# A SwiGLU down projection as seven block products, with the weights' sums made during the up projections

## The chip, the cores and the metric

One core of a Trainium2 chip runs one launch of the kernel. The metric is the device time of one execution in microseconds; lower is better. The time before is the median of three runs.

## The reference

Two layers of a decoder trunk with 512 tokens and a width of 1024, all in f32. In each layer one projection feeds four branches (a gated convolution, sparse attention with an indexer and a choice of the 128 best keys, a gated linear recurrence, and attention to 256 memory tokens). Each branch is lifted to the full width, gated and summed; an output projection and a residual follow, then a SwiGLU feed-forward network with a residual:

```python
x = x + merged @ w_out
hf = rmsnorm(x, norm_ffn)
gate, up = jnp.split(hf @ ffn_w_up, 2, axis=-1)        # 1024 -> 2 x 2816
return x + (jax.nn.silu(gate) * up) @ ffn_w_down        # 2816 -> 1024
```

The change is in the last line of the second layer: a product of (512 x 2816) with (2816 x 1024).

## The kernel before

**Precision.** TensorE multiplies in a rounded form of f32 (f32r). So each operand is split into a high part, a copy rounded by ScalarE (ACT, L97), and a low part, the difference that VectorE (DVE) takes. `mm3` (L271 to L276) makes of each block product three matmuls into one PSUM bank: high by high (L274), high by low (L275), low by high (L276).

**Weights.** `wchunk` (class `Chunk`, L212) loads up to 2048 columns per partition (1 MB) from DRAM by SP's queue into one of two `w_raw` buffers; ACT makes `w_hi` and DVE makes `w_lo` (L229) in parts of 1024 columns, three buffers of each. The profile calls both by these names.

**PSUM.** Eight banks of 128x512 f32: three for `mm` (projections), three for `tr` (transposes and norms) and two for `at` (attention). In the mixer `values` (L681) accumulates four token tiles at once and uses the three `mm` banks and one of `at`; meanwhile the attention's dots (L702, L703, exponentials on L715) use the `at` banks too.

**Order.** The program is written in Tile, and a planner with its own timeline of the engines sets the order of the instructions on each engine ahead of time. Each engine works off its list in order. `tc.high_priority` draws an instruction forward in the plan. Buffers and their semaphores order what the engines do with one another.

**The feed-forward network**, `ffn` (L1058). The hidden width of 2816 is 11 chunks of 256, in two parts of six and five chunks (each followed by its share of the down projection, so that the activations of one part fit in SBUF). For each chunk two 1 MB weight blocks make gate and up in feature-major form (96 matmuls of 128x512), DVE scales them by the norm as it evicts them (`fg`, `fu`, L1081), ACT applies Silu, DVE multiplies (L1086), and the product is split into `a_hi` (ACT) and `a_lo` (DVE, L1088).

The down projection of a part that isn't the last of layer 2 is `residual` (L1021): pairs of 128 output features, weights stationary, all chunks of the part accumulated in one bank for each, and added to `xT` (L1035), the residual stream that stays in SBUF, feature-major. In part 0 of layer 2 every finished feature block is also transposed (`transposed`, L1067) into `x_tok`, token-major. Part 1 of layer 2 is `final` (L1045): four token tiles by 512 columns accumulate in the three `mm` banks and one of `at`, activations stationary, are added to `x_tok` (L1051) and go out: the left 512 columns in one DMA (1 MB), the right ones in pieces of 128x256 by the queues of SP and ACT. In layer 1 the last part also spills x to DRAM (`x_spill`), from where the next mixer's end loads it again.

Of the kernel before, what the change touches and what calls it, by code (L numbers as in the profile page):

```python
# [12 lines left out]
F32 = mybir.dt.float32  # L13
F32R = mybir.dt.float32r
# [7 lines left out]
P = 128  # L22
# [47 lines left out]
def hybrid_trunk(ctx: ExitStack, tc: tile.TileContext, x, mem, positions, norm_mix, w_in, conv_w,  # L70
# [41 lines left out]
    def f(ap):  # L112
        return ap.bitcast(F32)

    ident = consts.tile([P, P], F32, name="ident")
    make_identity(nc, ident)
# [9 lines left out]
    dve.memset(one, 1.0)  # L126
    neg = consts.tile([P, P], F32, name="neg")
    dve.memset(neg, NONC)
# [141 lines left out]

    def mm3(ps, a, b, first, last):  # L271
        ah, al = a
        bh, bl = b
        pe.matmul(ps, ah, bh, start=first, stop=False)  # L274
        pe.matmul(ps, ah, bl, start=False, stop=False)  # L275
        pe.matmul(ps, al, bh, start=False, stop=last)  # L276

    x_dram = nc.dram_tensor("x_spill", [P, KD, S], F32, kind="Internal").ap()
    kv_dram = [nc.dram_tensor(f"kv{l}", [P, 4, 2, 2, MEM], F32, kind="Internal").ap() for l in range(DEPTH)]

# [21 lines left out]

    def column_means(ps, ones, sq, hi, lo):
        A(hi, sq, AF.Copy)
        dve.tensor_sub(lo, sq, f(hi))
        pe.matmul(ps, ones, hi, start=True, stop=False)
        pe.matmul(ps, ones, lo, start=False, stop=True)

    def norm_feature(ssq):
        ps = tr_ps()  # L310
        column_means(ps, ones_dr, ssq, *(scratch512(S).bitcast(F32R) for _ in range(2)))
# [172 lines left out]

    ones_dr = consts.tile([P, P], F32R, name="ones_dr")
    dve.tensor_copy(ones_dr, ones_d)
    ones_hr = consts.tile([P, P], F32R, name="ones_hr")
# [6 lines left out]
    a0, a1 = prm[:, 64:68], prm[:, 68:72]  # L494
    mx, e0, e1, sm, z0 = (small(H4, name=f"lb{i}", bufs=1) for i in range(5))
    dve.tensor_max(mx, a0, a1)
# [18 lines left out]

    def mixer(l, h, norms, cm, cf):
        mix = cm.enter_context(tc.tile_pool(name="mix", bufs=1, side="right"))
# [164 lines left out]
        def values(hv):  # L682
            ws = [wchunk(w_in[l][k0 * P:(k0 + 4) * P, C_GI:C_GI + 512], 4, 512) for k0 in (0, 4)]
            pss = [mm_ps() for _ in range(MM_BUFS)] + [at_ps()]
            tokens_wide(ws, h, KD, pss)
            for t, ps in enumerate(pss):
                with tc.high_priority(offset=AHEAD):
                    i = A(hv[:, t, :], ps, AF.Copy, scale=r_t[:, t:t + 1])
                if t < MM_BUFS:
                    behind.append(i)  # L690
            yield

        with pool_("dsa") as dp:
# [46 lines left out]
            with pool_("idx") as ip:  # L740
# [83 lines left out]
                def select(t):  # L824
                    n = (t + 1) * P
                    score = ip.tile([P, S], F32, name="score", bufs=1)[:, :n]
                    for hh in range(8):
# [9 lines left out]
                    dve.copy_predicated(score[:, t * P:], future, neg)  # L837
                    yield
# [22 lines left out]
                mgp = cf.enter_context(pool_("mgp", "left"))  # L861
                merged = mgp.tile([P, KD, S], F32, name="merged")
# [140 lines left out]

        res = cf.enter_context(tc.tile_pool(name="res", bufs=1))
        xT = res.tile([P, KD, S], F32, name="xT")
        for c in range(KD):
            nc.sync.dma_start(xT[:, c, :], x_dram[:, c, :])
        with pool_("outp") as op:
# [8 lines left out]
            residual(xT, w_out[l], mg, KD, 256, h2, ssq2, lambda c: g_ffn(l, c))  # L1017
        return h2, ssq2, xT

    def residual(xT, w2d, a, kt, cols, h2, ssq2, gain, spill=False, done=None):  # L1020
        for m0 in range(0, KD, cols // P):  # L1021
            ws = []
            k0 = 0
            per = 2048 // cols
            while k0 < kt:
                n = min(per, kt - k0)
                ws.append((k0, n, wchunk(w2d[k0 * P:(k0 + n) * P, m0 * P:m0 * P + cols], n, cols)))
                k0 += n
            pss = [mm_ps() for _ in range(cols // P)]
            for js in ([range(cols // P)] if m0 + cols // P < KD else [[j] for j in range(cols // P)]):  # L1030
                for k0, n, w in ws:
                    features(w, a, js, k0, kt, [pss[j] for j in js])
            for j in range(cols // P):
                m = m0 + j
                dve.tensor_add(xT[:, m, :], xT[:, m, :], pss[j])  # L1035
                if h2 is not None:
                    h_chunk(h2, ssq2, m, gain(m), xT[:, m, :])
                if spill:
                    nc.scalar.dma_start(x_dram[:, m, :], xT[:, m, :])
                if done is not None:  # L1040
                    done(m)

    def final(x_tok, w2d, a, kt):
        for m0 in range(0, D, 512):
            cols = slice(m0, m0 + 512)  # L1045
            ws = [wchunk(w2d[k0 * P:min(k0 + 4, kt) * P, cols], min(4, kt - k0), 512) for k0 in range(0, kt, 4)]
            pss = [mm_ps() for _ in range(MM_BUFS)] + [at_ps()]
            tokens_wide(ws, a, kt, pss)
            for t, ps in enumerate(pss):
                for c in ([cols] if m0 == 0 else [slice(m0 + e, m0 + e + 256) for e in (0, 256)]):  # L1050
                    dve.tensor_add(x_tok[:, t, c], x_tok[:, t, c], ps[:, c.start - m0:c.stop - m0])  # L1051
                    if m0:
                        q = nc.sync if c.start == m0 else nc.scalar
                        q.dma_start(out[0][t * P:(t + 1) * P, c], x_tok[:, t, c])
            if m0 == 0:
                nc.sync.dma_start(out[0][:, cols].rearrange("(t p) c -> p t c", p=P), x_tok[:, :, cols])

    def ffn(l, h, ssq, xT):  # L1058
        r_b = norm_feature(ssq)
# [3 lines left out]

        def transposed(m):
            ps = tr_ps()
            for t in range(NT):
                pe.transpose(ps[:, t * P:(t + 1) * P], xT[:, m, t * P:(t + 1) * P], ident)  # L1067
            A(x_tok[:, :, m * P:(m + 1) * P], ps.rearrange("p (a b) -> p a b", b=P), AF.Copy)

        with tc.tile_pool(name="ffn", bufs=1) as fp:  # L1070
            for f0, f1 in parts:
                kt = 2 * (f1 - f0)
                a = (fp.tile([P, 12, S], F32R, name="a_hi")[:, :kt], fp.tile([P, 12, S], F32R, name="a_lo")[:, :kt])
                for fc in range(f0, f1):
                    wg = wchunk(ffn_w_up[l][:, fc * 256:(fc + 1) * 256], KD, 256)
                    wu = wchunk(ffn_w_up[l][:, FF + fc * 256:FF + (fc + 1) * 256], KD, 256)
                    gs = [fp.tile([P, S], F32, name="fg", bufs=2) for _ in range(2)]
# [4 lines left out]
                    for j in range(2):  # L1082
                        i = 2 * (fc - f0) + j
                        g, u = gs[j], us[j]
                        A(g, g, AF.Silu)
                        dve.tensor_mul(g, g, u)  # L1086
                        A(a[0][:, i, :], g, AF.Copy)
                        dve.tensor_sub(a[1][:, i, :], g, f(a[0][:, i, :]))  # L1088
                wd = ffn_w_down[l][f0 * 256:f1 * 256, :]
                h2 = ssq2 = None  # L1090
                if last and f1 == n_f:
                    final(x_tok, wd, a, kt)
                    continue
                if f1 == n_f:
                    h2, ssq2 = new_h(), new_ssq()
                if last:
                    x_tok = fp.tile([P, NT, D], F32, name="x_tok")
                residual(xT, wd, a, kt, 256, h2, ssq2, lambda c: g_mix(l + 1, c), spill=h2 is not None,
                         done=transposed if last else None)
        return h2, ssq2  # L1100

    for l in range(DEPTH):
        with ExitStack() as ctx_ffn:
            with ExitStack() as ctx_mix:
                h, ssq, xT = mixer(l, h, (lambda: (norm_token(ssq), norm_feature(ssq))) if l else (lambda: norms),
                                   ctx_mix, ctx_ffn)
            h, ssq = ffn(l, h, ssq, xT)

# [28 lines left out]
```

## Time and profile before

| | us |
|---|---|
| median of 3 runs (lowest, highest) | 2047.54 (2046.99, 2047.55) |
| the profiled execution | 2047.71 |
| its span, first to last instruction | 2045.6 |
| layer 2, up projections of part 0 | from about 1687 to 1822 of the span |
| its down projection | to about 1887 |
| up projections of part 1 | to about 1987 |
| its down projection | to 2041.5 |
| last outputs | to 2045.6 |

A row of the profile has the start, the duration, the engine, the source line, the operation, what it writes and reads, and in brackets how long the engine had been idle and what released it. A group has count, total busy time, mean duration in ns, and the idle time before its instructions. A row of a DMA group has the queue, the count, the KB of each and the median microseconds from issue to landing. PE is TensorE, PEld its weight loads, POOL is GpSimd, SP is the engine whose queue loads the weights. The end of a matmul in the profile is modelled.

### The profile page before, as it was taken

Reading aid. Unit: us, or ns where it says so; the run is one execution under the profiler, and the core shown is the slowest. Engines: PE = TensorE matmul, PEld = TensorE weight load, DVE = VectorE, ACT = ScalarE, POOL = GpSimd, SP = SyncE. Lnnn points to the kernel's source line nnn. Section 1 sums busy time; section 2 is a strip of 40 time slices with the busy share of each in tenths; the row PEclk is TensorE's granted clock in tenths of the full one; section 3 lists DMA queues with packets and bytes.
Section 4 is the critical chain, followed back from the end, with each engine's and each line's share of the span. In section 5 each row is a group of like instructions: output and inputs, shape, how many; then the busy total and the mean of one; then the engine's idle time right before and its main releaser. Section 6 shows DMA issues by size and latency. Waiting matters only on the chain.

```text
span 2045.6 us, 26194 instructions
## 1 busy us (share of the span) xinstructions
PE 2031.7 (99%) x10156; PEld 1705.9 (83%) x10156; DVE 1277.0 (62%) x2519; ACT 1019.9 (50%) x1836; POOL 9.8 (0%) x33
## 2 busy tenths in 40 slices
PE   8999999999999999999999999999999999999999
PEld 8998987778888888888889898877888788888887
DVE  6779997657686544344457889864777654533442
ACT  7653655866665433223355456486766633322231
POOL 0000000000000000000000000000000000000000
PEclk9999999999999999999999999999999999999999
DMA  7623232212243232233243213222222422323222
GB/s 251 221 85 97 68 103 83 81 54 93 68 128 113 83 103 93 93 104 102 88 155 94 88 57 108 88 62 83 83 83 83 145 87 98 103 73 113 92 83 93
DMA packets 185660, 203.77 MB, mean 100 GB/s; under 512 B 4271, under 2 KB 172289, under 8 KB 185409
## 3 DMA queue, kind: packets, MB, share of 16 engines
q1 hardware_dynamic: 181248, 193.04, 29.7%
q10 hardware_dynamic: 4128, 8.93, 1.2%
q8 instruction: 80, 1.31, 0.3%
q14 instruction: 44, 0.35, 0.1%
q0 software_dynamic: 160, 0.13, 0.0%
HBM read 191.60 MB, written 10.49 MB: 99 GB/s over the span
## 4 chain that ended last, share of the span: by engine, by line
PE 97%; DMA 1%; DVE 1%; ACT 1%; issue 0%; SPq 0%; DVEq 0%
PE mm L274 29%; PE mm L275 29%; PE mm L276 29%; PE tr L732 1%; PE tr L726 1%; PE at L702 1%; PE at L703 1%; PE at L276 1%; PE at L274 1%; PE at L275 1%; DMA w_raw<-in_mem_w_kv_dram 1%; PE at L954 0%; PE at L980 0%; PE tr L668 0%; PE tr L771 0%
## 5 line engine op out<-in xcount | busy, mean ns | idle before, releaser
L229 DVE TENSOR_TENSOR w_lo<-w_raw,w_hi 128x1024 fp32r<-128x1024 f32 (+1 forms) x346 | 419.5, 1213 | 383.2 <-ACT w_hi L97 383.0
L274 PE MATMUL mm<-h_hi,w_hi 128*128 128x512 f32 x1664 | 651.9, 393 | 0.7 <-DVE fg L1081 0.4
L275 PE MATMUL mm<-h_lo,w_hi 128*128 128x512 f32 x1664 | 651.6, 392 | 0.0
L276 PE MATMUL mm<-h_hi,w_lo 128*128 128x512 f32 x1664 | 649.8, 392 | 0.0
L97 ACT ACTIVATE w_hi<-w_raw 128x1024 fp32r<-128x1024 f32 (+1 forms) x346 | 363.2, 1051 | 463.2 <-PE mm L275 397.5
L274 PEld LDWEIGHTS mm<-h_hi,w_hi 128*128 128x128 f32 x1664 | 313.2, 188 | 65.0 <-DVE fg L1081 1.2
L276 PEld LDWEIGHTS mm<-h_hi,w_lo 128*128 128x128 f32 x1664 | 312.9, 188 | 64.6 <-issue 0.6
L275 PEld LDWEIGHTS mm<-h_lo,w_hi 128*128 128x128 f32 x1664 | 313.1, 188 | 63.3 <-issue 1.0
L276 PE MATMUL mm<-w_hi,h_lo 128*128 128x256 f32 (+2 forms) x368 | 109.5, 298 | 0.0
L275 PE MATMUL mm<-w_lo,h_hi 128*128 128x256 f32 (+2 forms) x368 | 109.1, 297 | 0.0
L274 PE MATMUL mm<-w_hi,h_hi 128*128 128x256 f32 (+2 forms) x368 | 108.3, 298 | 0.0
L275 PE MATMUL mm<-a_lo,w_hi 128*128 128x512 f32 x272 | 106.1, 390 | 0.0
L274 PE MATMUL mm<-a_hi,w_hi 128*128 128x512 f32 x272 | 105.9, 389 | 0.0
L276 PE MATMUL mm<-a_hi,w_lo 128*128 128x512 f32 x272 | 105.6, 390 | 0.0
L274 PE MATMUL mm<-y_hi,w_hi 128*128 128x512 f32 x256 | 100.4, 393 | 1.2 <-ACT y_hi L97 1.2
L275 PE MATMUL mm<-y_lo,w_hi 128*128 128x512 f32 x256 | 100.7, 393 | 0.0
L276 PE MATMUL mm<-y_hi,w_lo 128*128 128x512 f32 x256 | 100.3, 392 | 0.0
L97 ACT ACTIVATE a_hi<-fg 128x512 fp32r<-128x512 f32 x44 | 27.8, 633 | 106.9 <-DVE fg L1086 106.9
L97 ACT ACTIVATE prob<-prob,small 128x256 f32<-128x256 f32 (+3 forms) x128 | 69.0, 554 | 14.7 <-DVE small L715 8.6
L275 PEld LDWEIGHTS mm<-w_lo,h_hi 128*128 128x128 f32 x368 | 70.2, 191 | 2.2
L276 PEld LDWEIGHTS mm<-w_hi,h_lo 128*128 128x128 f32 x368 | 70.2, 191 | 1.9
L274 PEld LDWEIGHTS mm<-w_hi,h_hi 128*128 128x128 f32 x368 | 69.9, 191 | 1.9
(377 smaller groups left out, 2982.9 us busy)
## 6 DMA issues: line engine op xcount, KB each, us to landing
w_raw<-in_w_in_dram SPq DMA_DIRECT2D x72, 1024.0 KB, 5.2
w_raw<-in_ffn_w_up_dram SPq DMA_DIRECT2D x44, 1024.0 KB, 5.1
w_raw<-in_w_lift_dram SPq DMA_DIRECT2D x32, 512.0 KB, 3.5
w_raw<-in_ffn_w_down_dram SPq DMA_DIRECT2D x16, 1024.0 KB, 5.3
w_raw<-in_mem_w_kv_dram SPq DMA_DIRECT2D x8, 1024.0 KB, 5.4
w_raw<-in_w_out_dram SPq DMA_DIRECT2D x8, 1024.0 KB, 5.4
w_raw<-in_ffn_w_down_dram SPq DMA_DIRECT2D x10, 512.0 KB, 3.4
kv<-kv ACTq DMA_DIRECT2D x8, 512.0 KB, 3.2
```

The lines of the kernel that those rows point to most:

```text
L97: i = act.activation(dst, src, func, **kw)
L229: dve.tensor_sub(lo, raw[:, k:e], f(hi))
L274: pe.matmul(ps, ah, bh, start=first, stop=False)
L275: pe.matmul(ps, ah, bl, start=False, stop=False)
L276: pe.matmul(ps, al, bh, start=False, stop=last)
L702: pe.matmul(ps, q[:, hh, s], k[0][:, :n], start=True, stop=False)
L703: pe.matmul(ps, q[:, hh, s], k[1][:, :n], start=False, stop=True)
L726: pe.transpose(pp[:, (2 * e + i) * P:(2 * e + i + 1) * P], probs[2 * i + e][:, b * P:(b + 1) * P], ident)
L732: pe.matmul(pv[e * HD:(e + 1) * HD, :], vt[:, b, :], pt[:, b, e * 2 * P:(e + 1) * 2 * P], start=b == 0, stop=b == t)
```

## The change

**Seven products.** Layer 2's down projection is computed for each chunk of 256 hidden features as a two-by-two block product: the activations as two halves of the tokens (256) by two halves of the chunk (128), the weights as two halves of the chunk by two halves of the columns (512). Eight block products become seven, on sums and differences of blocks: `A11`, `A12`, `A22`, `S1` to `S4` of the activations, and five of the weights' blocks and sums. Every block product is two token tiles of three matmuls of 128x512. The seven accumulate over all chunks of a part, in six banks (two `mm`, one `mm` with one `tr`, two `at`), in three phases; between the phases DVE adds banks into the output sum `acc`, and the accumulation goes on in the same bank where a later result contains an earlier one.

**Operands.** `operands` takes a chunk's two activation tiles and makes the seven blocks with their high and low parts. `weight_sums` loads the 256 rows of a chunk of `w_down` (1 MB) by POOL's queue into a third raw buffer, `w_raw7`, makes four sums in place on DVE and stores them in DRAM (`w_sums`), by POOL's queue again; one is made before each chunk's up projections. In the down projection SP's queue loads blocks of `w_down` and of `w_sums` into `w_raw` and `w_raw7` in turn.

**The residual stream.** x isn't held in SBUF through the network. The mixer's `residual` always spills it (ACT's queue); layer 1's down projection, `add_down`, loads each feature block by POOL's queue, adds and spills it again; layer 2 loads it in two 1 MB pieces into `w_raw7` by POOL's queue (`x_in`) and transposes it after chunks 1 and 3 of part 0.

**Banks.** `values` takes its fourth bank from `tr`.

Some constants are smaller, some pools lie elsewhere, and `fg` has three buffers. The core of the diff:

```diff
         def values(hv):
...
-            pss = [mm_ps() for _ in range(MM_BUFS)] + [at_ps()]
+            pss = [mm_ps() for _ in range(MM_BUFS)] + [tr_ps()]
...
+    def raw_tile(fp, turn=[0]):
+        turn[0] += 1
+        if turn[0] % 3 == 0:
+            return fp.tile([P, 2048], F32, name="w_raw7")
+        return wpool.tile([P, 2048], F32, name="w_raw", bufs=RAW_BUFS)
+
+    def split(srcs, earlier=()):
+        hi, lo = (wpool.tile([P, 2, 512], F32R, name=nm, bufs=W_BUFS) for nm in ("w_hi", "w_lo"))
+        with tc.high_priority(offset=AHEAD):
+            for k, n, src in srcs:
+                A(hi[:, k:k + n, :], src, AF.Copy)
+                follow(dve.tensor_sub(lo[:, k:k + n, :], src, f(hi[:, k:k + n, :])), earlier)
+        return [(hi[:, k, :], lo[:, k, :]) for k in range(2)]
+
+    def weight_sums(fp, w2d, i):
+        raw = fp.tile([P, 4, 512], F32, name="w_raw7")
+        nc.gpsimd.dma_start(raw.rearrange("p (e c) n -> p e (c n)", e=2),
+                            w2d[2 * i * P:2 * (i + 1) * P, :].rearrange("(e p) n -> p e n", p=P))
+        b12, b11, b22, b21 = (raw[:, j, :] for j in range(4))
+        dve.tensor_sub(b11, b12, b11)
+        dve.tensor_sub(b12, b22, b12)
+        dve.tensor_sub(b22, b22, b11)
+        dve.tensor_sub(b21, b21, b22)
+        nc.gpsimd.dma_start(wt_dram[:, i], raw)
+
+    def operands(fp, g0, g1):
+        hi, lo = (fp.tile([P, 7, HALF], F32R, name=nm, bufs=6) for nm in ("a_hi", "a_lo"))
+        def put(o, n, src):
+            h_, l_ = (x[:, o:o + n, :].rearrange("p a b -> p (a b)") for x in (hi, lo))
+            A(h_, src, AF.Copy)
+            dve.tensor_sub(l_, src, f(h_))
+        put(A11, 1, g0[:, :HALF])
+        put(A12, 2, g1)
+        dve.tensor_add(g0[:, HALF:], g0[:, HALF:], g1[:, HALF:])
+        dve.tensor_sub(g0[:, :HALF], g0[:, HALF:], g0[:, :HALF])
+        both = g1.rearrange("p (a b) -> p a b", b=HALF)
+        dve.tensor_sub(both, both, g0[:, None, :HALF].to_broadcast([P, 2, HALF]))
+        put(S2, 2, g0)
+        put(S4, 2, g1)
+        return hi, lo
+
+    def down(fp, w2d, sums, ops, evict):
+        n = len(ops)
+        b0 = mm_ps()
+        ba, bb, bc = [mm_ps(), mm_ps()], [b0, tr_ps()], [at_ps(), at_ps()]
...
+        for i0 in range(0, n, 2):
+            m = min(2, n - i0)
+            raw = raw_of(2 * m)
+            nc.sync.dma_start(raw, w2d[2 * i0 * P:2 * (i0 + m) * P, C1].rearrange("(k p) n -> p k n", p=P))
+            for i in range(m):
+                p1, p2 = split([(0, 2, raw[:, 2 * i:2 * i + 2, :])])
+                prod(ba, i0 + i, A11, p1, i0 + i == 0, i0 + i == n - 1)
+                prod(bb, i0 + i, A12, p2, i0 + i == 0, i0 + i == n - 1)
+        added = evict(ba, 0, C1) + evict(bb, 0, C1, True)
...
+        for i in range(n):
+            raw = raw_of(3)
+            nc.sync.dma_start(raw, sums[:, i, SUM1:])
...
+                todo = [(bc, S1, q5, j == 0, False), (ba, S2, q6, False, True), (bb, A22, q4, j == 0, False)]
...
+        added = evict(ba, 0, C2) + evict(bc, 2, C2)
+        later = added + evict(bb, 2, C1)
...
+            nc.sync.dma_start(raw[:, 0::2, :], sums[:, i0:i0 + m, SUM3])
+            nc.sync.dma_start(raw[:, 1::2, :], rows[:, i0:i0 + m, 1, C2])
...
+                p7, p3 = split([(0, 2, raw[:, 2 * i:2 * i + 2, :])], added if k == 1 else later if k else ())
+                prod(ba, k, S3, p7, False, k == n - 1, True)
+                late.append((bc, k, S4, p3, False, k == n - 1, True))
...
+        evict(ba, 2, C2, True)
+        evict(ba, 2, C1, True)
+        evict(bc, 0, C2, True, True)
...
+            def x_in(m0):
+                xs = fp.tile([P, 2048], F32, name="w_raw7")
+                nc.gpsimd.dma_start(xs.rearrange("p (m t) -> p m t", t=S), x_dram[:, m0:m0 + 4, :])
+                for m in range(4):
+                    ps = tr_ps()
+                    for t in range(NT):
+                        pe.transpose(ps[:, t * P:(t + 1) * P], xs[:, m * S + t * P:m * S + (t + 1) * P], ident)
+                    A(acc[:, :, (m0 + m) * P:(m0 + m + 1) * P], ps.rearrange("p (a b) -> p a b", b=P), AF.Copy)
...
+                if last:
+                    weight_sums(fp, ffn_w_down[l], f0)
                 for fc in range(f0, f1):
...
+                    ops.append(operands(fp, *gs))
...
+                    if fc in (1, 3):
+                        x_in(2 * fc - 2)
+                    if fc + 1 < f1:
+                        weight_sums(fp, ffn_w_down[l], fc + 1)
...
+                def evict(bank, t0, cols, done=False, tail=False):
+                    tail = final and tail
+                    adds = []
+                    with tc.high_priority(offset=2 * AHEAD):
+                        for t, ps in enumerate(bank):
+                            for w in (slice(0, 256), slice(256, 512)) if tail else (slice(0, 512),):
+                                c = slice(cols.start + w.start, cols.start + w.stop)
+                                d = acc[:, t0 + t, c]
+                                adds.append(dve.tensor_add(d, d, ps[:, w]))
+                                if final and done:
+                                    q = nc.scalar if tail and w.start else nc.sync if t0 or tail else nc.gpsimd
+                                    q.dma_start(out[0][(t0 + t) * P:(t0 + t + 1) * P, c], d)
+                    return adds
```

More of the change, by code (lines that the diff above doesn't have):

```diff
@@ L494, in hybrid_trunk @@
     a0, a1 = prm[:, 64:68], prm[:, 68:72]
-    mx, e0, e1, sm, z0 = (small(H4, name=f"lb{i}", bufs=1) for i in range(5))
+    mx, e0, e1, sm, z0 = (small(H4) for _ in range(5))
     dve.tensor_max(mx, a0, a1)
@@ new lines, in hybrid_trunk, with follow @@
+    HALF = S // 2
+    A11, A12, A22, S2, S1, S4, S3 = range(7)
+    C1, C2 = slice(512, 1024), slice(0, 512)
+    def raw_tile(fp, turn=[0]):
[3 more added lines that the diff above has]
+        return wpool.tile([P, 2048], F32, name="w_raw", bufs=RAW_BUFS)
+    def follow(i, earlier):
+        for e in earlier:
+            tc.add_manual_dep(i.ins, e.ins.name, order, reason="additions first")
+    def split(srcs, earlier=()):
[5 more added lines that the diff above has]
+        return [(hi[:, k, :], lo[:, k, :]) for k in range(2)]
@@ L1093, in ffn @@
                     continue
[L1094 to L1099, printed above, removed]
+                def evict(bank, t0, cols, done=False, tail=False):
+                    tail = final and tail
+                    adds = []
+                    with tc.high_priority(offset=2 * AHEAD):
+                        for t, ps in enumerate(bank):
+                            for w in (slice(0, 256), slice(256, 512)) if tail else (slice(0, 512),):
[6 more added lines that the diff above has]
+                    return adds
```

171 lines of the change are left out of this document (102 added, 69 removed).

## The prediction

> **What bounds the kernel now.** I read the page first, for the engines' shares and the chain that ended last.
>
> ```profile
> span 2045.6 us, 26194 instructions
> PE 2031.7 (99%) x10156; PEld 1705.9 (83%) x10156; DVE 1277.0 (62%) x2519; ACT 1019.9 (50%) x1836; POOL 9.8 (0%) x33
> PEclk9999999999999999999999999999999999999999
> PE 97%; DMA 1%; DVE 1%; ACT 1%; issue 0%; SPq 0%; DVEq 0%
> ```
>
> TensorE is busy for 99% of the span, the chain that ended last is 97% PE, and the granted clock is full in every slice. So time is counted in matmuls: one that goes is worth its issue time, and work on other engines is free until it makes PE wait. Busy time doesn't price a matmul, because matmuls overlap. The timeline does; here are the first and the last of 34 consecutive matmuls of layer 2's down projection.
>
> ```profile
> 2033.77 0.39 PE L276 MATMUL mm<-w_hi,a_lo 128*128 128x512 f32 x1
> ...
> 2041.25 0.39 PE L276 MATMUL at<-w_hi,a_lo 128*128 128x512 f32 x1
> ```
>
> Each shows 0.39 us, but the 33 steps between their starts take 7.48 us: 0.2267 us each. Then the table by stage: columns are window, length, then busy time and instructions of PE, weight loads, DVE, ACT and POOL, granted clock, DMA share, GB/s.
>
> ```profile
> 1687.00:1822.00 135.00, 134.80 (x595) 111.28 (x594) 63.45 (x75) 44.60 (x53) 0.00 (x0) 1.00 0.29 93
> 1822.00:1885.00 63.00, 63.00 (x295) 52.15 (x294) 18.40 (x20) 16.23 (x19) 0.00 (x0) 1.00 0.30 101
> 1987.00:2041.00 54.00, 54.00 (x240) 44.71 (x239) 16.82 (x22) 9.12 (x9) 0.00 (x0) 1.00 0.23 78
> ```
>
> These are layer 2's up projections of part 0 (six chunks, 576 matmuls and the end of the output projection), most of part 0's down, and part 1's down: 240 matmuls in 54.0 us, 0.225 each, which confirms the price. PE never stops in either down stage, while DVE works 63.45 of 135 us in the up stage and 18.40 of 63 in the down stage: there is room beside PE.
>
> **The change, part by part.**
>
> *Seven products.* Layer 2's down has 11 chunks of 256 rows. Before, each takes 48 matmuls of 128x512 (two row blocks, eight blocks of output, three products of halves): 528. After, seven half-size products for each chunk, each over two banks with three matmuls: 42, together 462. The built order of the changed kernel has these 462, of the same shape, and the other PE instructions are as many as before. 66 go: 66 x 0.2267 = **-15.0 us**. The 32 transposes of x stay, in another place.
>
> *Feeding the down stage.* A chunk now takes raw blocks of 0.5 MB (phase 1), 0.75 MB (phase 2, sums from DRAM) and 0.5 MB (phase 3), 1.835 million bytes in 42 x 0.2267 = 9.52 us: 193 GB/s, against 101 and 78 above. Is that too much for three raw buffers? The nearest stage is the start-up, which loads 1 MB blocks into two.
>
> ```profile
> 30.00:50.00 20.00, 20.00 (x173) 20.00 (x172) 15.39 (x33) 15.91 (x42) 0.00 (x0) 1.00 0.75 251
> w_raw<-in_ffn_w_down_dram SPq DMA_DIRECT2D x16, 1024.0 KB, 5.3
> w_raw<-in_ffn_w_down_dram SPq DMA_DIRECT2D x10, 512.0 KB, 3.4
> L97 ACT ACTIVATE w_hi<-w_raw 128x1024 fp32r<-128x1024 f32 x338 | 357.2, 1058 | 451.6 <-PE mm L275 388.2 <-PE mm L276 29.0 <-PE at L276 19.8
> L229 DVE TENSOR_TENSOR w_lo<-w_raw,w_hi 128x1024 fp32r<-128x1024 f32 x338 | 412.8, 1222 | 377.7 <-ACT w_hi L97 377.5
> ```
>
> It moves 251 GB/s and PE is busy for all 20 us. A 0.75 MB load lies between 3.4 and 5.3 us, 4.4 by their middle. With three buffers up to two loads are under way while the third is used, and each of phase 2's loads has 18 matmuls, 4.1 us, of its own to work beside and those of the load ahead of it: by my count of the built order the tightest may take 6.5 us before PE waits. A pair of blocks gives PE 12 matmuls, 2.72 us, and costs ACT 1.06 and DVE 1.22. So 0 us; if that slack of 2 us is gone, each of phase 2's 11 loads could cost up to 1 us, which is a rival below.
>
> *Evictions between the phases.* At a phase change DVE adds four banks into the output sum before it splits the next weights. The nearest row is the residual's add of one bank.
>
> ```profile
> L1035 DVE TENSOR_TENSOR xT<-xT,mm 128x512 f32<-128x512 f32 x40 | 27.4, 686 | 42.9 <-PE mm L276 42.8
> ```
>
> 4 x 0.69 = 2.76 us. Behind them in DVE's queue stand splits, and behind those PE; split pairs already made last PE 2.72 us each, and three buffers hold up to two ahead, so 2.76 is mostly covered. Bounds: 0, and 4 changes x 2.76 = 11.0. I take **+1.0**, near the lower end.
>
> *More on DVE in the up stage.* Per chunk come four subtractions for the weight sums (4 x 0.69 = 2.8 us) and the activations' combinations, 2.6 us net of the two old splits: +5.4. For six chunks 63.45 + 32 = 96 of 135 us, 71%: free as an average. The tight place is the norm at the head of the stage, where PE's first eviction waits for DVE.
>
> ```profile
> 1691.47 1.23 DVE L229 TENSOR_TENSOR w_lo<-w_raw,w_hi 128x1024 fp32r<-128x1024 f32 x1 [6.09 <-ACT w_hi L97]
> ```
>
> DVE has been idle for 6.09 us before 1691.47, and the first sums (2.8 us), whose load waits only for the output projection's buffers, fit there. 0; if that load is late, 2.8 at once.
>
> *The POOL queue.* Every weight-sum chunk is loaded by POOL's queue into one buffer (1 MB), subtracted in place, stored by the same queue (1 MB), and the next load waits for that store; two 1 MB loads of x use the same buffer in part 0. PE's transposes of x stand in its in-order queue after chunks 1 and 3, with 192 matmuls (43.5 us) between, and in that time the buffer must see five of these DMAs and eight subtractions (5.5 us): d, the time of one, may be up to (43.5 - 5.5) / 5 = 7.6 us. Beyond, PE waits, and the first-phase loads behind the part's last store as well: I count some 12 of part 0's 14 DMAs on the path, so about 12 us for every microsecond of d over 7.6. What is d? The trace has no large DMA on this queue, only small ones.
>
> ```profile
> gq_raw<-in_dsa_q_norm_dram POOLq DMA_DIRECT2D x2, 32.0 KB, 5.0
> 1.34 0.71 POOL L182 DMA_DIRECT2D gq_raw<-in_dsa_q_norm_dram  x1 [0.34 <-issue]
> ```
>
> Lower bound: 5.3, the same megabyte on SP's queue. Upper: 5.0 + 5.3 = 10.3, if all that the 32 KB show is overhead that comes on top. But those ran in the start-up's crowd, and POOL itself takes 0.71 us to issue one, so I take 6.5, near the lower end. Cost at 6.5: **0**; at 10.3: 2.7 x 12 = +32.
>
> The Trainium skill has a rule against exactly this. Its page "SBUF — State Buffer", section "SBUF: two separate sides", warns that DMAs issued from the GpSimd queue starve for descriptors while VectorE runs an operation in its two-port mode; the section after it states some 620 ns growing to 3100 ns, which as an estimate would put 2.5 us on each DMA, 9.0 in all, and the time at about 2051. No run here shows it yet. Whether the rule applies hangs on the mode of the subtractions beside these DMAs: their 1222 ns for 1024 elements is the pace of the add with an operand in PSUM (686 ns for 512), so I see no faster mode in them.
>
> *Values' fourth bank.* Before, values take the fourth bank from the two `at` banks, and the attention's dots have one left:
>
> ```profile
> PE at L702 <- DVE small L715: 2.4, 6, 0.4
> 333.02 0.22 PE L702 MATMUL at<-k_hi,qS 128*128 128x128 f32 x1
> 333.75 0.33 PE L702 MATMUL at<-k_hi,qS 128*128 128x128 f32 x1 [0.39 <-DVE small L715]
> 334.58 0.33 PE L702 MATMUL at<-k_hi,qS 128*128 128x128 f32 x1 [0.39 <-DVE small L715]
> ```
>
> Dots follow each other at 0.83 us where their two matmuls need about 0.3: six gaps of 0.53, 3.2 us. In the built order two dots come earlier and five run in turn over two banks; I halve it, **-1.6** (bounds -3.2, and +0.7 for a transpose that waits one eviction of 0.69 for its bank).
>
> *The tail.* Before, one of the last four banks after the other is finished, and only one add is left when PE stops:
>
> ```profile
> 2040.32 0.75 DVE L1051 TENSOR_TENSOR x_tok<-x_tok,mm 128x256 f32<-128x256 f32 x2 [0.61 <-PE mm L276]
> 2041.68 0.75 DVE L1051 TENSOR_TENSOR x_tok<-x_tok,at 128x256 f32<-128x256 f32 x2 [0.61 <-PE at L276]
> out_dram<-x_tok SPq DMA_DIRECT2D x4, 128.0 KB, 1.8
> ```
>
> The last add ends 2042.43, 1.18 us after the last matmul's start, and the last output takes the 3.2 us to the end of the span. In the built order the last four banks end 6, 4, 2 and 0 matmuls before the end. DVE has four adds of 0.69 and four of 0.375, 4.26 us, and can begin 0.94 us before the last matmul is issued: 3.33 us after it instead of 1.18, **+2.2**; with 1.5 MB of outputs queued in those few microseconds it may be +3.5.
>
> *The rest.* x always goes back to DRAM (ACT's queue, issues that block no computation) and comes back by POOL's queue in layer 1 (256 KB, four buffers, a pair used every 72 matmuls, 16.3 us, or 60 matmuls, 13.6 us): 10.3 us at the upper bound above is still covered. Smaller constants and pools moved: 0.
>
> Sum: -15.0 + 1.0 - 1.6 + 2.2 = -13.4. The profiled execution took 2047.71 us (2.1 outside its span), 0.2 above the median of the runs; 2047.71 - 13.4 = 2034.3, as a median **2034**.
>
> **The rivals.**
>
> *POOL's chain sets part 0* (the other side). The place is x's second transposes and the loads behind the last store; the price is 12 us per microsecond of d above 7.6. One way to get there: each of these DMAs waits out two of DVE's subtractions, 2 x 1.22, before it moves, d = 8.9, +16 us: 2050 (the page above names such a lock). It eats the 13.4 us at d = 8.7; at 8.0 the time is 2039, at 10.3 it is 2066. For it: 5.0 us for 32 KB. Against it: the size of that DMA is no part of those 5.0. Slower than before by over 0.2%, or nearly so, 0.08; between 7.6 and 8.7 another 0.05.
>
> *The down stage starves.* 193 GB/s in short loads, some waiting for the third buffer, cost 5 to 10 us: 2039 to 2044. For it: twice the present rate; against: the 251 GB/s above. 0.09.
>
> *A matmul is worth its 0.39 us*, so 66 save 25.7: 2047.5 - 25.7 + 1.6 = 2023. The start spacing speaks against it: 0.02.
>
> *The change doesn't take the matmuls away*: the built order rules that out.
>
> **How the numbers follow.** The forecast has 0.76: from the terms' ends, 2031 (values' full 3.2, no eviction stall, and a little) to 2038. With the starving case the range is 2031 to 2044; outside are mostly POOL's chain near and beyond break-even and the 0.39 case. A measurement tells 0.2%, 4.1 us, from no change: faster (below 2043.4) are the forecast's 0.76, 0.02 and 0.08 of the starving and POOL cases' low ends, 0.86; within 0.2% are their rest, 0.06; slower 0.08.
>
> **What would show it.** Right: part 0's down in 57 to 59 us (252 matmuls at 0.2267 are 57.1; before 288 are 65.3) and part 1's in 48 to 49 (210 are 47.6; before 54.4), no PE wait over 2 us at the transposes of x, 1 MB DMAs on POOL's queue at 5.3 to 7.6 us, dots' waits halved, last add 3.3 us after the last matmul. Wrong: PE waiting for DMA at the transposes of x or at the first phase's loads (POOL's chain); waits of PE for `w_hi` or `w_lo` all through the down stages (starving); a matmul spacing above 0.2267 there.

## The result, and the profile after

| | before | changed |
|---|---|---|
| median, us (lowest to highest, 4 runs each) | 2047.26 (2046.31 to 2047.55) | 2038.62 (2037.88 to 2039.48) |
| the profiled execution | 2047.71 | 2037.88 |
| its span | 2045.6 | 2036.2 |

The ratio is 0.9961, with a 95% interval from 0.9949 to 0.9973: faster by more than 0.2%. But 8.6 us were gained where 13.4 were forecast. The time lies inside the range of 2031 to 2044, yet above 2038, the upper end that the forecast's own terms gave: the part of the range that holds it was put there for a starving down stage, which the profile doesn't show. That it lies inside is luck. The page of the changed kernel, first for what should be as forecast:

```profile
span 2036.2 us, 26441 instructions
PE 2017.4 (99%) x10090; PEld 1692.7 (83%) x10090; DVE 1356.6 (67%) x2653; ACT 1046.3 (51%) x1880; POOL 34.7 (2%) x75
PE 93%; DMA 3%; DVE 2%; ACT 1%; issue 1%; SPq 0%; DVEq 0%; ACTq 0%
```

10090 matmuls instead of 10156 are the 66. PE is still 99% of the span. The stages of the two down projections (columns as in the prediction's table of windows) and the DMAs that the change adds:

```profile
1829.00:1886.00 57.00, 57.00 (x254) 47.18 (x253) 36.64 (x45) 21.61 (x24) 1.67 (x3) 1.00 0.61 203
1981.00:2029.00 48.00, 48.00 (x213) 39.77 (x212) 30.28 (x39) 18.97 (x22) 1.10 (x2) 1.00 0.44 145
```

```profile
w_raw<-in_ffn_w_down_dram POOLq DMA_DIRECT2D x11, 1024.0 KB, 6.1
w_sums<-w_raw POOLq DMA_DIRECT2D x11, 1024.0 KB, 5.2
w_raw<-x_spill POOLq DMA_DIRECT2D x2, 1024.0 KB, 5.6
w_raw<-w_sums SPq DMA_DIRECT2D x11, 768.0 KB, 5.7
```

PE never stops in either down projection, at 203 GB/s. POOL's queue takes 6.1 us for a load and 5.2 for a store, where I took 6.5 for both. The Trainium skill's page "DMA: Bandwidth & Descriptors", section "Measured (HBM→SBUF, 128 partitions, SWDGE, issued from GpSimd)", has 6.15 us for 1 MB, but of the DMA engines' busy time alone; the 6.1 here runs from issue to landing, so the two are close without being the same quantity.

So where did 4.8 us go? To find that, the kernel is cut at a matmul which both have, the first of layer 2's up projections that waits for the norm; first the row of the kernel before, then two of the changed one, the cut and the last matmul.

```profile
1694.80 0.50 PE L274 MATMUL mm<-h_hi,w_hi 128*128 128x512 f32 x1 [0.20 <-DVE fg L1081]
```

```profile
1697.86 0.50 PE L275 MATMUL mm<-h_hi,w_hi 128*128 128x512 f32 x1 [0.18 <-DVE fg L1208]
2029.74 0.39 PE L277 MATMUL at<-w_hi,a_lo 128*128 128x512 f32 x1
```

| stretch | before | changed | difference | forecast |
|---|---|---|---|---|
| start to the cut | 1694.80 | 1697.86 | +3.06 | -1.6 |
| the cut to the last matmul | 346.45 | 331.88 | -14.6 | -14.0 |
| last matmul's start to the end of the span | 4.35 | 6.46 | +2.1 | +2.2 |
| the span | 2045.6 | 2036.2 | -9.4 | -13.4 |

The profiled executions differ by up to 2.1 us within their first 200 matmuls, while the first loads arrive; so smaller differences at the cut mean little.

Layer 2's network and the tail came out as forecast. The loss lies ahead of the cut, in attention code of which the change seems to touch one line. The waits of PE, by the view that groups them, of the changed kernel (engine, line, releaser: total, times, longest):

```profile
PE at L702 <- DVE small L715: 3.5, 5, 2.9
...
PE mm L275 <- ACT y_hi L97: 1.2, 1, 1.2
...
PE mm L276 <- DVE w_lo L230: 0.8, 1, 0.8
```

One wait of 2.9 us stands at the very dots that were to gain. Its place in the timeline of the changed kernel, PE and then DVE:

```profile
334.60 0.39 PE L277 MATMUL tr<-w_hi,h_lo 128*128 128x512 f32 x1
337.86 0.33 PE L702 MATMUL at<-k_hi,qS 128*128 128x128 f32 x1 [2.87 <-DVE small L715]
...
336.46 0.68 DVE L842 MATCH_REPLACE8 score<-m,score 128x512 f32<-128x512 f32 x1
337.17 0.43 DVE L845 TENSOR_SCALAR bias<-score 128x512 f32<-128x512 f32 x1
337.51 0.28 DVE L715 CUSTOM_DVE_ANT_0 prob<-at,causal_bias 128x128 f32<-128x128 f32 x1
```

Values are done (the last matmul into `tr` starts at 334.60), both `at` banks are full of dots drawn ahead, and DVE is still in the selection of the best keys, without a gap; only when that ends (L845, 337.17) does it come to empty a bank. In the kernel before that row stands at 331.76, ahead of the dots.

The wait isn't all. The prediction read the row of nines as a full clock, but a 9 there is any share from 90% up, of a slice of 51 us. By windows (columns as in the prediction's table) the granted clock is 0.50 in a stretch of 3.4 us that begins 1.8 us behind this wait, and also in one of the kernel before, at 336 us. First the changed kernel, then the kernel before, then e2 (below), which has no such stretch in layer 1:

```profile
339.70:343.10 3.40, 3.40 (x10) 2.72 (x11) 3.40 (x8) 0.91 (x6) 0.00 (x0) 0.50 0.08 10
```

```profile
336.00:339.40 3.40, 3.40 (x10) 2.66 (x9) 3.29 (x10) 2.66 (x11) 0.00 (x0) 0.50 0.11 13
```

```profile
339.70:343.10 3.40, 3.40 (x16) 2.82 (x16) 0.00 (x0) 0.83 (x3) 0.00 (x0) 1.00 1.03 348
```

Matmuls of 128x512 start 0.43 us apart in it instead of 0.23, some eight of them, so each such stretch costs about 1.6 us. All eight profiled kernels with a wait of 2.9 us or more at layer 1's dots have 3.4 to 10.2 us at half clock there; of the six without it only the kernel before has any. That the wait brings the half clock is argued from this; no run separates the two.

### The profile page after: what moved, and what is told of

It reads as the page before. It is cut to its first block, busy times and chain, and to the rows that moved or that the text cites. A ratio compares the mean times of both kernels' runs of the same rounds, so it can differ in the third digit from the quotient of the medians.

```text
span 2036.2 us, 26441 instructions
## 1 busy us (share of the span) xinstructions
PE 2017.4 (99%) x10090; PEld 1692.7 (83%) x10090; DVE 1356.6 (67%) x2653; ACT 1046.3 (51%) x1880; POOL 34.7 (2%) x75
## 4 chain that ended last, share of the span: by engine, by line
PE 93%; DMA 3%; DVE 2%; ACT 1%; issue 1%; SPq 0%; DVEq 0%; ACTq 0%
PE mm L275 28%; PE mm L276 27%; PE mm L277 27%; DMA w_raw<-in_ffn_w_down_dram 1%; PE tr L732 1%; PE at L702 1%; PE tr L726 1%; DMA w_sums<-w_raw 1%; PE at L703 1%; PE at L275 1%; PE at L277 1%; PE at L276 1%; DMA w_raw<-in_mem_w_kv_dram 1%; PE tr L275 0%; PE tr L276 0%
## 5 line engine op out<-in xcount | busy, mean ns | idle before, releaser
L97 ACT ACTIVATE w_hi<-w_raw 128x1024 fp32r<-128x1024 f32 (+2 forms) x368 | 381.5, 1039 | 410.0 <-PE mm L276 313.1
L230 DVE TENSOR_TENSOR w_lo<-w_raw,w_hi 128x1024 fp32r<-128x1024 f32 (+1 forms) x324 | 392.4, 1213 | 282.3 <-ACT w_hi L97 281.4
L97 ACT ACTIVATE a_hi<-fg 128x512 fp32r<-128x512 f32 (+1 forms) x66 | 39.3, 596 | 111.0 <-DVE fg L1211 96.6
L1068 DVE TENSOR_TENSOR w_lo<-w_raw,w_hi 128x1024 fp32r<-128x1024 f32 (+1 forms) x44 | 47.6, 1090 | 37.1 <-ACT w_hi L97 37.1
L275 PE MATMUL mm<-a_hi,w_hi 128*128 128x512 f32 x176 | 68.5, 389 | 0.0
L276 PE MATMUL mm<-a_lo,w_hi 128*128 128x512 f32 x176 | 68.5, 389 | 0.0
```

Of the source, the lines that this page charges most:

```text
L97: i = act.activation(dst, src, func, **kw)
L230: dve.tensor_sub(lo, raw[:, k:e], f(hi))
L275: pe.matmul(ps, ah, bh, start=first, stop=False, skip_group_check=more)
L276: pe.matmul(ps, ah, bl, start=False, stop=False, skip_group_check=more)
L1068: follow(dve.tensor_sub(lo[:, k:k + n, :], src, f(hi[:, k:k + n, :])), earlier)
```

## The experiments

Times are medians; the ratio's interval is against the kernel before, run beside each.

### Does the wait belong to the bank?

Three kernels: the changed one with the old bank, the kernel before with the new one, and the changed one with the new bank in layer 2 only.

```diff
 e1, on the changed kernel
-            pss = [mm_ps() for _ in range(MM_BUFS)] + [tr_ps()]
+            pss = [mm_ps() for _ in range(MM_BUFS)] + [at_ps()]
 e2, on the kernel before
-            pss = [mm_ps() for _ in range(MM_BUFS)] + [at_ps()]
+            pss = [mm_ps() for _ in range(MM_BUFS)] + [tr_ps()]
 e3, on the changed kernel
-            pss = [mm_ps() for _ in range(MM_BUFS)] + [tr_ps()]
+            pss = [mm_ps() for _ in range(MM_BUFS)] + [tr_ps() if l else at_ps()]
```

> The changed kernel, with the values' fourth bank taken from `at` again. The changed kernel's profile shows one wait of 2.9 us at layer 1's dots, where forecast and trace differ most. Theory A: the wait belongs to the bank; two dots are drawn ahead into the two free `at` banks while VectorE is still in the selection, and the third stands in TensorE's queue until VectorE comes. Then the wait goes here, the six gaps of about 0.5 us come back, and the time falls by 1 to 2 us below the changed kernel (about 2037). Rival B: the planner's order puts VectorE's selection later in any case, whatever the bank: the wait stays and the time is the changed kernel's, within 0.5 us, or above it.

> The kernel before, with only the values' fourth bank taken from `tr`. Theory A: the same long wait appears at layer 1's dots, layer 2's gaps shrink by 0.8 us, and the time is 0 to 2 us above the kernel before. Rival B (the long wait comes from another part of the change): both layers gain, 1.6 us below the kernel before (2045.7), as the prediction had it.

> The changed kernel, with the fourth bank from `at` in layer 1 and from `tr` in layer 2 only. Theory A: layer 1 loses the 2.9 us wait and gets its three gaps back, layer 2 keeps its gain: 1.5 to 2.5 us below the changed kernel, 2036 to 2037. Rival B: as the changed kernel, 2038.6.

| | us | ratio (interval) | layer 1's selection ends (L845) | the cut |
|---|---|---|---|---|
| e1 | 2041.80 | 0.9973 (0.9963 to 0.9983) | 336.37 | 1699.67 |
| e2 | 2043.10 | 0.9984 (0.9975 to 0.9992) | 332.49 | 1691.18 |
| e3 | 2038.82 | 0.9961 (0.9948 to 0.9975) | 338.04 | 1701.34 |

Theory A falls three times (e1's runs spread from 2038.57 to 2043.92; none comes down to 2037). With the old bank the wait stays (first fence: e1's waits); with the new one alone it isn't there (second: e2's).

```profile
PE at L702 <- DVE small L715: 5.1, 6, 3.1
```

```profile
PE at L702 <- DVE small L715: 0.7, 4, 0.2
```

The bank alone saves 3.3 us (3.6 at the cut), more than the 1.6 forecast. The six gaps shrink to 0.17 or vanish, and PE's waits at the dots fall by 1.7 us (2.4 to 0.7), as forecast; in the profiles another 1.6 us is the stretch at half clock, which e2 doesn't have. Rival B holds: something else makes DVE late.

### Which line makes VectorE late?

I compared DVE's lists of instructions as built. Of the first 800 of the kernel before, the changed kernel has 529 in the same order, and 759 if one line is put back: the computation of the gates' lower bounds takes its five 128x4 tiles from the shared pool `small` (twelve buffers in rotation) instead of buffers of their own. In time, the first of those instructions in the kernel before and in the changed one:

```profile
8.96 0.16 DVE L496 TENSOR_TENSOR lb<-prm 128x4 f32<-128x4 f32 x1 [0.82 <-ACT prm L97]
```

```profile
74.75 0.15 DVE L496 TENSOR_TENSOR small<-prm 128x4 f32<-128x4 f32 x1
```

In the start-up DVE has idle time for them (0.82 us ahead of this one); at 75 us it is in the mixer's work.

```diff
 e6, on the changed kernel (e7: the reverse, on the kernel before)
-    mx, e0, e1, sm, z0 = (small(H4) for _ in range(5))
+    mx, e0, e1, sm, z0 = (small(H4, name=f"lb{i}", bufs=1) for i in range(5))
```

> The changed kernel, with one line put back: the five small tiles of the gates' lower bounds (`mx`, `e0`, `e1`, `sm`, `z0`) have buffers of their own again instead of five turns of the shared `small` pool. The bank change alone (e2) came 3.3 us below the kernel before and had no long wait at layer 1's dots, and the changed kernel with the old bank (e1) kept the wait: the wait belongs to something else. Theory C: this line. With shared buffers VectorE's list of layer 1 is another one from its sixteenth instruction on, the selection of the keys ends 5 us later, and TensorE waits at the dots. Then the wait goes here, layer 1 ends about 6 us earlier than in the changed kernel, and the time is 2032 to 2033.5. Rival D: another part of the change that lies ahead of layer 1's attention (the mean's scale moved into the split, the broadcast constant): 2038, as the changed kernel.

> The kernel before, with only that line changed: the five small tiles from the shared pool. Theory C: the 2.9 us wait at layer 1's dots appears, the matmuls of layer 1's end stand 4 to 5 us later than before, and the time is 2050.5 to 2052. Rival D: as before, 2047.

e6 took 2036.88 (0.9952, 0.9939 to 0.9964), e7 took 2059.95 (1.0065, 1.0053 to 1.0078). e6's selection ends at 331.86, its dots wait as in e2:

```profile
PE at L702 <- DVE small L715: 0.7, 4, 0.2
```

In e7 the long wait appears, as theory C has it:

```profile
PE at L702 <- DVE small L715: 5.0, 6, 3.1
```

So the line does make the wait. But both times missed: e6 gave 1.7 us and not 6, e7 cost 13 and not 4 to 5. At the 2000th matmul (about 339 us) e6 is 5.5 us ahead of the changed kernel, 336.17 against 341.71, near the forecast, though 1.5 us of this arose in the first 200 matmuls; at the cut it is behind, 1697.99. Against the kernel before, e7 loses 5.3 us between the 200th and the 2100th matmul, as forecast, and 7.5 more up to the cut. No wait accounts for the later losses. Consecutive matmuls of the output projection do, first and last of ten steps, in the kernel before and in e6:

```profile
679.78 0.39 PE L274 MATMUL mm<-mg_hi,w_hi 128*128 128x512 f32 x1
...
682.04 0.39 PE L275 MATMUL mm<-mg_lo,w_hi 128*128 128x512 f32 x1
```

```profile
679.74 0.39 PE L275 MATMUL mm<-mg_hi,w_hi 128*128 128x512 f32 x1
...
682.07 0.39 PE L276 MATMUL mm<-mg_lo,w_hi 128*128 128x512 f32 x1
```

2.26 us before, 2.33 in e6, for the same kind of matmuls. Only the matmuls that read `y` (the lifts, 768) or `mg` (the output projection, 384) are slower; those on `h` keep their 227 ns.

### Why do the same matmuls get slower?

`y` and `mg` are allocated from the right end of SBUF, `w_hi`, `w_lo` and `h` from the left, behind the constants. Each of the five tiles takes 32 bytes per partition, so e6 and e7 shift everything behind them on the left by 160 bytes, e6 up and e7 down. The change itself adds an unused tile of 128 bytes, "spacer".

```diff
 e10, on e8 (below)
-    consts.tile([P, 128], U8, name="spacer")
+    consts.tile([P, 96], U8, name="spacer")
 e11, on the kernel before, ahead of the first constant
+    consts.tile([P, 64], U8, name="spacer")
```

> As e8 (own buffers for the five small tiles, fixed order of the last matmuls), with the spacer at the head of the constants 96 bytes long instead of 128. In e6 and e8 the wait at layer 1's dots was gone, 6 us, but the matmuls that read y and merged (1152 in all) went from 227 to 231, 232 and 237 ns each and gave most of it back. The five tiles had moved every tile behind them on the left side by 160 bytes, while y and merged lie at the right side and had stayed. Theory E: the step of a matmul depends on the distance of its stationary and its moving operand in SBUF, modulo 128 bytes; 96 bytes in place of 128 make it a multiple of 128 again (96 past one on both sides). Then those matmuls take 227 ns, and the time is e8's less 5 to 6 us: 2029.5 to 2031. Rival F: the slower matmuls belong to the order or to other traffic: as e8, 2035.6.

> The kernel before, with 64 unused bytes at the head of the constants and nothing else: every tile of the left side moves by 64 bytes, y and merged stay; the instruction lists are the same. Theory E: the 1152 matmuls on y and merged take some 7 ns more each, about 234, and the time is 8 us above the kernel before (2055). Rival F: 2047, as before.

e11 took 2052.96 (1.0027, 1.0018 to 1.0037), 5.5 us above its 2047.41: 64 unused bytes, with the instruction lists unchanged, make the kernel slower. The ten steps in e11:

```profile
679.67 0.39 PE L276 MATMUL mm<-mg_lo,w_hi 128*128 128x512 f32 x1
...
682.00 0.39 PE L277 MATMUL mm<-mg_hi,w_lo 128*128 128x512 f32 x1
```

2.33 us again, and no wait is new. That the address decides is shown; so rival F falls. `h` and `w_hi` have moved together and keep their pace, so what counts is the distance and not the place. The size was 8 forecast, 5.5 measured: the mean step without waits rises from 226.7 to 233.3 ns on `mg` and from 228.0 to 233.3 on `y`, 6.4 us in all and not 8, and e11's profile lacks the stretch at half clock of the kernel before (1.6 us).

e10 took 2035.04 (0.9938, 0.9926 to 0.9951), 0.6 below e8 and not 5: its ten steps are still 2.34 us.

```profile
679.56 0.39 PE L277 MATMUL mm<-mg_hi,w_lo 128*128 128x512 f32 x1
...
681.90 0.39 PE L275 MATMUL mm<-mg_hi,w_hi 128*128 128x512 f32 x1
```

So the modulus of theory E is wrong. By the addresses in the built kernels, the distance from the first `w_hi` (left) to `y_hi` (right), and its remainder, which `mg` shares, are:

| kernel | distance, bytes | past a multiple of 256 | ten steps, us |
|---|---|---|---|
| before | 105216 | 0 | 2.26 |
| changed | 106240 | 0 | 2.27 |
| e6 | 106080 | 96 | 2.33 |
| e7 | 105376 | 160 | 2.34 |
| e10 | 106112 | 128 | 2.34 |
| e11 | 105152 | 192 | 2.33 |

A multiple of 256 fits all six, and the eight other kernels built here: on `mg`, the seven at 0 step at 226.7 ns and e8, at 96, at 233.3. A larger modulus isn't needed: in the kernel before, the matmuls on `h` stand at multiples of 512, those on `y` and `mg` 256 past one, and both step at 227. If it is 256, a spacer of 224 bytes in e10 would bring the distance to a multiple again, and by e2's cut (1691.18 against e10's 1696.82) be worth up to 5.6 us more. That was not tried.

### The tail

```diff
 e5, on the changed kernel (cut short); e8 is e5 with e6's line
+                if k == n - 1:
+                    for t in range(2):
+                        for bank, j, o, b, start, stop, more in late:
+                            run_.append(mm3(bank[t], ...))          # one bank after the other
+                    for x, y in zip(run_, run_[1:]):
+                        follow(y[0], [x[2]])                        # order only, behind P7's matmuls
```

> The changed kernel, with the order of the last matmuls fixed: the two `mm` banks end 18 matmuls before the end, then one `at` bank's nine matmuls, then the other's nine. The prediction charged 2.2 us to the tail, because four banks end within six matmuls. If the additions on VectorE set it, the last addition ends 1.2 us after the last matmul's start instead of 2.9, and the time falls by 1.5 to 2 us (2036.8). Rival: the outputs' DMAs set the end (1.5 MB within the last microseconds), and the time falls by less than 0.7.

> The changed kernel with both: own buffers for the five small tiles, and the order of the last matmuls fixed as in e5. The two lie far apart in time, so the gains should add: e5 took 2.9 us off, theory C says 6 us off, 2029 to 2031. Rival D: 2035.7, as e5.

e5 took 2035.71 (0.9946, 0.9934 to 0.9959), 2.9 below the changed kernel; e8 2035.61 (0.9948, 0.9934 to 0.9961). DVE's last rows, of the changed kernel and of e5:

```profile
2028.80 2.48 DVE L1241 TENSOR_TENSOR acc<-acc,mm 128x512 f32<-128x512 f32 x4 [4.48 <-PE mm L277]
2031.20 1.41 DVE L1241 TENSOR_TENSOR acc<-acc,at 128x256 f32<-128x256 f32 x4
```

```profile
2026.07 2.48 DVE L1251 TENSOR_TENSOR acc<-acc,mm 128x512 f32<-128x512 f32 x4 [1.08 <-PE mm L277]
2028.79 0.75 DVE L1251 TENSOR_TENSOR acc<-acc,at 128x256 f32<-128x256 f32 x2 [0.24 <-PE at L277]
2030.83 0.75 DVE L1251 TENSOR_TENSOR acc<-acc,at 128x256 f32<-128x256 f32 x2 [1.29 <-PE at L277]
```

In the changed kernel eight additions run in one go and end 2.87 us after the last matmul's start (2032.61 against 2029.74); in e5 they are spread over the last 18 matmuls, and two are left after it. Last matmul to end of the span: 6.46 us before the edit, 4.0 in e5 (2030.41 to 2034.4). The additions set this part of it, not the outputs' DMAs. e8 is no better than e5: its `y` and `mg` matmuls are slow, as in e6.

### How much room did the feeding have?

```diff
 e9, on the changed kernel, in weight_sums: the load twice
+        nc.gpsimd.dma_start(raw..., w2d[...])
         nc.gpsimd.dma_start(raw..., w2d[...])
 e12, on the changed kernel, in down's phase 2
+            nc.sync.dma_start(raw[:, 2:3, :], sums[:, i, SUM4:])
             nc.sync.dma_start(raw, sums[:, i, SUM1:])
 e13, on the changed kernel, in down's phase 2
-                todo = [(bc, S1, q5, ...), (ba, S2, q6, ...), (bb, A22, q4, ...)]
+                todo = [(bc, S1, q5, ...), (ba, S2, q6, ...)] + ([(bb, A22, q4, ...)] if j in (0, n - 1) else [])
```

> The changed kernel, with the 1 MB load of each weight-sum chunk issued twice into the same buffer, so that POOL's chain is longer by one DMA per chunk. The changed kernel's DMAs took 6.1 (load), 5.2 (store) and 5.6 us (x), 5.7 on average. Theory of the prediction (the chain becomes the bound when the five DMAs between x's two transposes and their subtractions pass 43.5 us): now 2 x 12.2 + 2 x 5.2 + 5.6 + 5.5 = 45.9, a wait of 2 us or more at the second transposes, and part 0's whole chain about as long as its up projections; 2 to 6 us above the changed kernel. Rival: the chain has more room than counted, no wait, within 0.7 us of the changed kernel.

> The changed kernel, with a third of each phase-2 load (256 KB) issued once more ahead of the whole (768 KB) into the same buffer, so that the whole waits for it. The load took 5.7 us in the changed kernel, where the prediction had estimated 4.4 and a limit of 6.5. If that limit is right, a load of 8 to 9 us makes TensorE wait up to 2 us at each of 11 loads: 5 to 20 us above the changed kernel. Rival: the three buffers hide more than counted, within 1.5 us of the changed kernel.

> The changed kernel without the seventh product (A22 with the fourth sum) in all chunks but the first and the last of each part: 7 chunks x 6 = 42 matmuls less, which leaves that part of the result out; loads, splits and additions stay. By the prediction's price a matmul that goes is worth its 0.2267 us: 9.5 us below the changed kernel (2029.1). Rival (the down stage starves): phase 2 then asks for 768 KB in every 2.72 us, 289 GB/s, and waits for its loads give part of it back, less than 7 us below.

e9 took 2067.91 (1.0100, 1.0086 to 1.0113), 29 us above the changed kernel, where 2 to 6 were expected and the rival expected none: POOL's chain is a real limit, and nearer than counted. PE waits once, at the first phase of part 0's down, whose third load needs the buffer of the last sums; last store, and the first matmul after the wait:

```profile
1843.45 0.55 POOL L1085 DMA_DIRECT2D w_sums<-w_raw  x1 [8.03 <-DVE w_raw L1084]
...
1854.12 1.65 PE L275 MATMUL mm<-w_hi,a_hi 128*128 128x512 f32 x3 [26.82 <-ACT w_hi L97]
```

The granted clock is 0.50 behind this wait too, for 5.2 us with 12 matmuls, which makes the other 2.5 of the 29 us:

```profile
1854.10:1859.30 5.20, 5.18 (x12) 4.11 (x13) 3.50 (x3) 1.87 (x2) 0.00 (x0) 0.50 0.34 92
```

The last store comes at 1806.66 in the changed kernel. Six more loads made it 36.8 us later, 6.1 each, and 26.8 of these are PE's wait: the chain had 10 us of room. The planner had moved x's transposes out of the way, so that place, on which the estimate of 7.6 rested, was not the first to give.

e12 took 2037.87 (0.9951, 0.9938 to 0.9963), as the changed kernel: its two loads take 4.4 and 4.2 us, one behind the other, and PE is busy for all 57 us of the stage. e13, which leaves out part of the result, took 2027.65 (0.9901, 0.9887 to 0.9914), 11.0 below it; by the profiled spans, 2036.2 and 2026.2, it is 10.0, where 42 x 0.2267 make 9.5. The down stage doesn't starve, not even where phase 2 asks for half as much data again in the same time.

## Why the prediction was right, and where it was not

**Seven products: right.** -14.6 us with the evictions in them, against -15.0 + 1.0. PE never waits in the down stages, and e13 shows what one more product's matmuls are worth. The eviction term was 0 rather than 1.0; the missing 0.4 is one wait in the up projections of part 1, which the prediction doesn't have:

```profile
1952.97 0.50 PE L275 MATMUL mm<-h_hi,w_hi 128*128 128x512 f32 x1 [0.18 <-DVE fg L1208]
```

**Feeding: right in effect, sizes off both ways.** The 768 KB loads took 5.7 us, not 4.4, and the limit of 6.5 that I named doesn't exist: e12's path of 8.6 costs nothing. POOL's DMAs took 5.2 to 6.1; 10 us of room over the part's 14 DMAs put the edge at 5.7 + 10 / 14 = 6.4 us each, an estimate from e9, and not at 7.6. The rival stood closer than its 0.13. The rule on VectorE's lock (the Trainium skill's page "SBUF — State Buffer", section "SBUF: two separate sides") did not bite: beside DVE's subtractions the medians stayed at 5.2 to 6.1 us, where it would have made some 9.

**Values' bank: right sign, half the size.** -3.3 us alone (e2), at the end of the bounds. That it meets the unhalved 3.2 is chance: the gaps gave 1.7, which is the forecast, and the clock at the dots, which the prediction took for full, about as much again in the profiles. In the changed kernel the gain is buried under the wait.

**Tail: right.** +2.1 against +2.2, and 1.7 of it by the mechanism named (the last addition ends 2.87 instead of 1.18 us after the last matmul's start); the other 0.4 lies between that addition and the end of the span. e5 takes it back.

**The rest, 0: wrong, and this is the miss.** "Smaller constants and pools moved: 0" held one line, five tiny tiles moved to a shared pool, that moves DVE's whole list. At the cut the bank alone gives -3.6 (e2), the changed kernel has +3.06: 6.7 us lost. Of these 4.6 are this line by layer 1's dots (e6 against the changed kernel, from the 200th to the 2100th matmul): 2.8 of shorter waits there and about 1.6 of the stretch at half clock behind them. How the rest divides between the later order of layer 1 and layer 2 is open, since every kernel that puts the line back also moves the addresses. I had looked for what the edit adds to each engine (nothing), and not at where the built list first differs. Nor did I look for short stretches of a lower clock, which the row of nines hides.

Sum by the trace: -14.6 + 2.1 - 3.6 + 6.7 = -9.4.

## What to carry to other kernels

Where a planner orders the instructions, an edit that costs nothing by itself still isn't free: look for the first place where each engine's list differs, and ask whether that edit explains it. Rotating buffers couple work that has nothing to do with one another; tiny start-up values want buffers of their own. And when a kernel with the same instructions takes another time and shows no wait, compare the steps of equal matmuls before looking for anything else, then the granted clock by short windows, and then the addresses of their operands.

## What the runs showed of the hardware

A matmul's step depends on where its operands lie. The same 128x512 matmuls took 227 ns where the two tiles from which they read lay a multiple of 256 bytes apart, and 233 to 234 on average at 96, 128, 160 and 192 bytes past one. The distance alone doesn't set how much: in e6 the matmuls on `mg` and `w_lo` take 237, the others 231 and 232. 64 unused bytes cost the kernel 5.5 us (e11). Without its spacer of 128 bytes the changed kernel would have a distance of 106368, 128 past a multiple; this may be why it carries one, but no run leaves the spacer out. The Trainium skill's page "SBUF — State Buffer", section "A bandwidth-pool intuition that's wrong (but worth ruling out)", gives TensorE an independent second read port for weight loads; here the port isn't independent of the address, or something else is shared. Which of the two it is stays open.

Behind a wait of PE the granted clock can be lower: it was 0.50 for 3.4 us behind the 2.87 us at layer 1's dots, and for 5.2 us behind e9's 26.8, with matmuls 0.43 us apart instead of 0.23.
